# The low parts of the attention weights: an accumulating DMA in place of a GpSimd subtraction

## The chip, the cores and the metric

The kernel runs on one core of one Trainium2 chip. The metric is the device time of one execution in microseconds (us), as the median of several runs. Five engines are spoken of: TensorE (PE in the profile, with PEld for its loading of weights), VectorE (DVE), ScalarE (ACT), GpSimd (POOL) and SyncE (SP), which issues DMA transfers. Each engine works through its own list of instructions in order.

## The reference

The program is a first transformer block (sparse attention beside a gated linear recurrence, then a feed-forward network) followed by two layers of a second block (feed-forward, four mixers, feed-forward), on 512 tokens of width 1024 in float32. What matters for this change is that it is a long sequence of products of the tokens with weights that are each used once, and that between some of them stand attention stages:

```
h = _rmsnorm(x, norm1_g)
proj = h @ w_in
...                                  # queries, keys, values, gates, recurrence
attn = _nsa(q, k_cmp, v_cmp, k_slc, kv[:, :, 3], k_win, kv[:, :, 5], nsa_g)
merged = merge_g[:, :, 0] * (attn @ w_o_attn) + merge_g[:, :, 1] * (lru @ w_o_lru)
x = x + merged @ w_out
...
for l in range(DEPTH_2):
    x = x + 0.5 * swiglu(rms_norm(x, ffn1_norm[l]), ffn1_w_gate[l], ffn1_w_up[l], ffn1_w_down[l])
    h = rms_norm(x, mix_norm[l])
    pa, pb, pc, pd = jnp.split(h @ w_in[l], IN_SPLITS, axis=-1)
    ...                              # four mixers: ya, yb, yc, yd
    x = x + jnp.concatenate([ya, yb, yc, yd], axis=-1) @ w_out[l]
    x = x + 0.5 * swiglu(rms_norm(x, ffn2_norm[l]), ffn2_w_gate[l], ffn2_w_up[l], ffn2_w_down[l])
    x = rms_norm(x, final_norm[l])
```

## The kernel before

Float32 products are made of three products in the type float32r, which TensorE takes at its full rate: a number is split into a high part `hi` (the number rounded to float32r) and a low part `lo` (the number less `hi`), and the product is x_hi·w_hi + x_lo·w_hi + x_hi·w_lo. These are the three matmuls on lines 150 to 152 (`feat`, weights as the stationary or loaded operand) and on lines 180 to 182 (`tok_`, tokens as the rows of the result).

Weights come through `stream` (line 116). A DMA on SP's queue (line 126) loads four slices of 128x256, 512 KB, into a tile `raw`, of which there are two in turn. For each half of it, ScalarE writes `hi` (line 133) and another engine writes `lo` as `raw` less `hi` (line 135). There are four `hi` and four `lo` tiles in turn, so that one call of `stream` with eight slices fills the whole ring; the next call's first tile has to wait until TensorE has read the tile four places before it. A `raw` tile is free for the next load when both of its halves have been split.

Which engine writes `lo` hangs on `self.attends`. It is false in the feed-forward networks, the merge and the output projection, where VectorE does it. It is true in the three attention stages, where POOL does it: the loop over 32 units of head and branch in `nsa` (from line 1644), and the loop over 16 heads in `mix` (from line 563 to 1292), which runs once in each of the two layers. In these stages projections, gates and output projections for what comes next are put between the steps of the heads: `Fill.pump` issues them one slice at a time, at lower priority. A head's step is: scores on TensorE, minimum or maximum on VectorE, exponential on ScalarE, reciprocal on VectorE, scaling on POOL (lines 782, 958, 1106, 1585), transposes on TensorE, a split by ScalarE and VectorE (lines 219, 220), and the product with the values on TensorE.

The order of the instructions on each engine is set by a scheduler when the program is built. It goes by priorities (`tc.high_priority`: a weight load is moved up by 6000, its split by 3000, fills are moved back by 300) and by a timeline that it models. A changed instruction can therefore change the order of others.

Of the kernel before, what the change touches and what calls it, by code (L numbers as in the profile page):

```python
# [8 lines left out]
FT = mybir.dt.float32  # L9
FR = mybir.dt.float32r  # L10
I32 = mybir.dt.int32
AF = mybir.ActivationFunctionType
OP = mybir.AluOpType
# [79 lines left out]
class Kern:  # L93
# [22 lines left out]
    def stream(self, src, K, C):  # L116

        nc, tc = self.nc, self.tc
        parts = []
        st = max(1, min(4, 1024 // C))  # L120
        sp = max(1, st // 2)
        for h in range(0, K, st):
            n = min(st, K - h)
            raw = self.wp.tile([128, 1024], FT, tag="raw", name="raw", bufs=2)
            with tc.high_priority(offset=6000):
                nc.sync.dma_start(raw[:, :n * C], src[:, h * C:(h + n) * C])
            for i in range(0, n, sp):
                c = min(sp, n - i) * C
                hi = self.wp.tile([128, 512], FR, tag="hi", name="hi", bufs=self.wb)
                lo = self.wp.tile([128, 512], FR, tag="lo", name="lo", bufs=self.wb)  # L130
                x = raw[:, i * C:i * C + c]
                with tc.high_priority(offset=3000):
                    nc.scalar.activation(hi[:, :c], x, AF.Copy)  # L133
                    eng = nc.gpsimd if self.attends else nc.vector
                    eng.tensor_tensor(lo[:, :c], x, hi[:, :c].bitcast(FT), op=OP.subtract)  # L135
                for j in range(min(sp, n - i)):
                    parts.append((hi, lo, j * C))

        def get(k, a=0, b=C):
            hi, lo, o = parts[k]  # L140
            return hi[:, o + a:o + b], lo[:, o + a:o + b]
        return get
# [1690 lines left out]
```

## Time and profile before

| what | us |
|---|---|
| median of 3 runs (lowest, highest) | 3132.08 (3131.34, 3133.15) |
| the profiled execution, own time | 3132.92 |
| its span | 3131.1 |
| PE busy in the span | 3030.5 |
| VectorE, ScalarE, POOL busy in the span | 1721.3, 1389.4, 736.7 |

The 1.8 us between the profiled execution's time and its span lie outside the recorded program. The busy shares are means over the whole span: 97% for PE, 55% for VectorE, 44% for ScalarE and 24% for POOL. POOL's work is nearly all in the three attention stages, so its share has to be read stage by stage. The stretches used here for the stages are 100 to 500 us (first block), 1390 to 1760 us and 2400 to 2760 us (the mixers of the two layers). Granted clock is the share of full speed that TensorE was given.

### The profile page before, as it was taken

The page shows a single profiled execution, that of the slowest core. Times are in us where ns is not written, and L with a number is a line of the kernel's source. Part 1 is how long each engine was busy: PE and PEld are TensorE (multiplying, and loading weights), DVE is VectorE, ACT ScalarE, POOL GpSimd, SP SyncE. Part 2 cuts the span into 40 slices and gives each one's busy share as a digit, 9 for nine tenths or more (in the row PEclk, how much of TensorE's full clock was granted, in tenths as well). Part 3 has the DMA queues.
Part 4 walks back from the last instruction along what each step waited for, and adds up shares of the span by engine and source line. Part 5 has one row for each costly group of instructions (what it writes and reads, how often), then busy time and mean ns, then how long its engine had stood idle before and what let it go on. Part 6 is the DMA issues. An engine that isn't in the chain of part 4 may idle for free.

```text
span 3131.1 us, 41177 instructions
## 1 busy us (share of the span) xinstructions
PE 3030.5 (97%) x15289; PEld 2549.3 (81%) x15289; DVE 1721.3 (55%) x3167; ACT 1389.4 (44%) x2707; POOL 736.7 (24%) x699
## 2 busy tenths in 40 slices
PE   7999999999999999999888999999999998999998
PEld 6888877888888888889877888888888987778886
DVE  7576785454444454337786554355443488665433
ACT  4577774343333333236765333333332577543322
POOL 0466650010000000028853000010000877210000
PEclk9999999999999999999989999999999998999999
DMA  4311112342333323333211323323233321122232
GB/s 135 105 60 58 48 41 76 100 143 95 100 98 91 101 95 95 101 112 100 79 32 41 101 95 98 99 89 99 97 96 97 111 90 47 41 88 94 95 101 81
DMA packets 105265, 275.81 MB, mean 88 GB/s; under 512 B 27172, under 2 KB 36900, under 8 KB 104904
## 3 DMA queue, kind: packets, MB, share of 16 engines
q1 hardware_dynamic: 105064, 273.18, 28.1%
q8 instruction: 120, 1.97, 0.3%
q14 instruction: 81, 0.66, 0.1%
HBM read 268.93 MB, written 6.80 MB: 88 GB/s over the span
## 4 chain that ended last, share of the span: by engine, by line
PE 73%; issue 13%; DVE 7%; ACT 3%; POOL 3%; DMA 1%; SPq 0%; DVEq 0%; POOLq 0%; ACTq 0%
PE ps_mm L150 7%; PE ps_mm L152 7%; PE ps_mm L151 7%; PE ps_s L151 6%; PE ps_s L150 6%; PE ps_s L152 6%; PE ps_t L152 6%; PE ps_t L150 6%; PE ps_t L151 6%; PE ps_mm L180 2%; PE ps_mm L181 2%; PE ps_mm L182 2%; DVE PTl L220 1%; PE ps_t L792 1%; POOL lo L135 1%
## 5 line engine op out<-in xcount | busy, mean ns | idle before, releaser
L133 ACT ACTIVATE hi<-raw 128x512 fp32r<-128x512 f32 (+4 forms) x952 | 594.5, 627 | 1362.0 <-PE ps_mm L151 410.5
L135 DVE TENSOR_TENSOR lo<-raw,hi 128x512 fp32r<-128x512 f32 (+1 forms) x782 | 547.0, 701 | 934.1 <-ACT hi L133 925.5
L150 PE MATMUL ps_mm<-xh,hi 128*128 128x512 f32 x784 | 309.8, 395 | 1.4 <-ACT hi L133 1.2
L152 PE MATMUL ps_mm<-xh,lo 128*128 128x512 f32 x784 | 307.0, 394 | 3.1 <-POOL lo L135 3.1
L151 PE MATMUL ps_mm<-xl,hi 128*128 128x512 f32 x784 | 307.7, 392 | 0.0
L233 POOL TENSOR_TENSOR acc<-acc,sq 128x512 f32<-128x512 f32 x42 | 62.5, 1488 | 1037.8 <-issue 525.7
L152 PE MATMUL ps_s<-xh,lo 128*128 128x512 f32 (+1 forms) x664 | 259.7, 392 | 6.3 <-DVE lo L135 6.3
L150 PE MATMUL ps_s<-xh,hi 128*128 128x512 f32 (+1 forms) x664 | 256.9, 392 | 7.4 <-ACT hi L133 7.4
L151 PE MATMUL ps_s<-xl,hi 128*128 128x512 f32 (+1 forms) x664 | 260.6, 392 | 3.0 <-DVE xl L238 2.9
L181 PE MATMUL ps_mm<-lo,xh 128*128 128x256 f32 (+1 forms) x896 | 255.9, 288 | 2.0 <-DVE lo L135 2.0
L180 PE MATMUL ps_mm<-hi,xh 128*128 128x256 f32 (+1 forms) x896 | 255.4, 289 | 1.3 <-ACT tk L661 1.0
L182 PE MATMUL ps_mm<-hi,xl 128*128 128x256 f32 (+1 forms) x896 | 253.7, 286 | 0.1
L135 POOL TENSOR_TENSOR lo<-raw,hi 128x512 fp32r<-128x512 f32 (+2 forms) x170 | 225.5, 1334 | 114.6 <-ACT hi L133 107.9
L150 PE MATMUL ps_t<-xh,hi 128*128 128x512 f32 x608 | 236.9, 390 | 0.0
L151 PE MATMUL ps_t<-xl,hi 128*128 128x512 f32 x608 | 236.7, 389 | 0.0
L152 PE MATMUL ps_t<-xh,lo 128*128 128x512 f32 x608 | 235.9, 390 | 0.3 <-DVE lo L135 0.3
L152 PEld LDWEIGHTS ps_mm<-xh,lo 128*128 128x128 f32 x784 | 148.2, 189 | 35.1 <-POOL lo L135 4.1
L180 PEld LDWEIGHTS ps_mm<-hi,xh 128*128 128x128 f32 x896 | 171.9, 193 | 5.0 <-issue 1.7
L181 PEld LDWEIGHTS ps_mm<-lo,xh 128*128 128x128 f32 x896 | 172.5, 193 | 4.0 <-DVE lo L135 2.5
L150 PEld LDWEIGHTS ps_mm<-xh,hi 128*128 128x128 f32 x784 | 148.6, 190 | 32.9 <-ACT hi L133 1.9
L182 PEld LDWEIGHTS ps_mm<-hi,xl 128*128 128x128 f32 x896 | 171.9, 193 | 1.7 <-DVE xl L238 0.5
L151 PEld LDWEIGHTS ps_mm<-xl,hi 128*128 128x128 f32 x784 | 148.7, 190 | 30.1
(526 smaller groups left out, 6646.7 us busy)
## 6 DMA issues: line engine op xcount, KB each, us to landing
raw<-in_w_g SPq DMA_DIRECT2D x110, 512.0 KB
raw<-in_w_u SPq DMA_DIRECT2D x110, 512.0 KB
raw<-in_w_d SPq DMA_DIRECT2D x108, 512.0 KB
raw<-in_w_o SPq DMA_DIRECT2D x24, 512.0 KB
raw<-in_w_c SPq DMA_DIRECT2D x16, 512.0 KB
raw<-in_w_m SPq DMA_DIRECT2D x16, 512.0 KB
raw<-in_w_a SPq DMA_DIRECT2D x12, 512.0 KB
raw<-in_w_d SPq DMA_DIRECT2D x20, 256.0 KB
```

What stands on the lines that cost most here:

```text
L133: nc.scalar.activation(hi[:, :c], x, AF.Copy)
L135: eng.tensor_tensor(lo[:, :c], x, hi[:, :c].bitcast(FT), op=OP.subtract)
L150: mm(ps, wh, mh(km), start=s, stop=False)
L151: mm(ps, wh, ml(km), start=False, stop=False)
L152: mm(ps, wl, mh(km), start=False, stop=e)
L180: mm(out[tb], h, wh, start=k == 0 and tb % 2 == 0, stop=False)
L181: mm(out[tb], h, wl, start=False, stop=False)
L182: mm(out[tb], o, wh, start=False, stop=k == K - 1 and tb % 2 == 1)
L220: self.nc.vector.tensor_sub(lo, src, hi.bitcast(FT))
L233: (eng or nc.gpsimd).tensor_tensor(acc, acc, sq, op=OP.add)
L792: PE.transpose(ps[:, qb * 128:qb * 128 + 128], P[qb][:, kb * 128:kb * 128 + 128], ident)
```

## The change

Where `self.attends` is true, POOL's subtraction is taken out. ScalarE writes a second time from `raw`, with the scale -1.0, into `lo`, which then holds the negated high part. A DMA issued on POOL's queue then adds `raw` to `lo` in place (`accum_op=OP.add`). In the other stages nothing is changed in the source.

```diff
--- before.py
+++ after.py
@@ -131,8 +131,11 @@
                 x = raw[:, i * C:i * C + c]
                 with tc.high_priority(offset=3000):
                     nc.scalar.activation(hi[:, :c], x, AF.Copy)
-                    eng = nc.gpsimd if self.attends else nc.vector
-                    eng.tensor_tensor(lo[:, :c], x, hi[:, :c].bitcast(FT), op=OP.subtract)
+                    if self.attends:
+                        nc.scalar.activation(lo[:, :c], x, AF.Copy, scale=-1.0)
+                        nc.gpsimd.dma_start(lo[:, :c], x, accum_op=OP.add)
+                    else:
+                        nc.vector.tensor_sub(lo[:, :c], x, hi[:, :c].bitcast(FT))
                 for j in range(min(sp, n - i)):
                     parts.append((hi, lo, j * C))
```

The lines below 134 move down by up to three; the added DMA is line 136. The places below are in the first block's attention, where the projection of the recurrence for the next head group is filled in. In these rows `hi`, `lo` and `raw` are the weights' tiles, and the numbers count the program's tiles, so that the same tile has another number in the two programs: `hi_3386`, `hi_3390`, `hi_3396`, `hi_3400` before are `hi_3414`, `hi_3419`, `hi_3426`, `hi_3431` now; the low part's number is one higher.

ScalarE's list before at this refill of the ring (P: exponentials of the softmax, PTh: high parts of the transposed probabilities):

```order
L133 ACTIVATE hi_3386<-raw_3384 128x512
L133 ACTIVATE hi_3390<-raw_3384 128x512
L219 ACTIVATE PTh_2737<-ps_t_2734 128x256
L219 ACTIVATE PTh_2765<-ps_t_2763 128x128
L219 ACTIVATE bdh_3643<-bdr_3641 128x512
L1583 ACTIVATE P2_3025,st4_2960<-P2_3025,st4_2960 128x384
L133 ACTIVATE hi_3396<-raw_3394 128x512
L133 ACTIVATE hi_3400<-raw_3394 128x512
```

ScalarE's list now at the same place:

```order
L133 ACTIVATE hi_3414<-raw_3412 128x512
L1586 ACTIVATE P0_2988,st4_2984<-P0_2988,st4_2984 128x128
L135 ACTIVATE lo_3415<-raw_3412 128x512
L222 ACTIVATE PTh_2757<-ps_t_2754 128x256
L133 ACTIVATE hi_3419<-raw_3412 128x512
L135 ACTIVATE lo_3420<-raw_3412 128x512
L133 ACTIVATE hi_3426<-raw_3424 128x512
L135 ACTIVATE lo_3427<-raw_3424 128x512
L222 ACTIVATE bdh_3675<-bdr_3673 128x512
L1586 ACTIVATE P2_3049,st4_2984<-P2_3049,st4_2984 128x384
L222 ACTIVATE PTh_2785<-ps_t_2783 128x128
```

Three writes of a low part stand among the writes of the high parts, each in front of softmax work that was next in the list before.

TensorE's list before, from the first use of the ring's first tile to the first use of the second tile's low part:

```order
L150 MATMUL ps_mm_3405<-xh_96,hi_3386 128x512
L151 MATMUL ps_mm_3405<-xl_97,hi_3386 128x512
L152 MATMUL ps_mm_3405<-xh_96,lo_3387 128x512
L150 MATMUL ps_mm_3405<-xh_96,hi_3386 128x512
L151 MATMUL ps_mm_3405<-xl_97,hi_3386 128x512
L152 MATMUL ps_mm_3405<-xh_96,lo_3387 128x512
L150 MATMUL ps_mm_3405<-xh_96,hi_3390 128x512
L151 MATMUL ps_mm_3405<-xl_97,hi_3390 128x512
L152 MATMUL ps_mm_3405<-xh_96,lo_3391 128x512
```

TensorE's list now, from inside the first tile's use to the first use of the second tile's low part:

```order
L155 MATMUL ps_mm_3437<-xh_96,lo_3415 128x512
L153 MATMUL ps_mm_3437<-xh_96,hi_3419 128x512
L154 MATMUL ps_mm_3437<-xl_97,hi_3419 128x512
L153 MATMUL ps_mm_3438<-xh_96,hi_3414 128x512
L154 MATMUL ps_mm_3438<-xl_97,hi_3414 128x512
L155 MATMUL ps_mm_3438<-xh_96,lo_3415 128x512
L153 MATMUL ps_mm_3438<-xh_96,hi_3414 128x512
L154 MATMUL ps_mm_3438<-xl_97,hi_3414 128x512
L155 MATMUL ps_mm_3438<-xh_96,lo_3415 128x512
L153 MATMUL ps_mm_3438<-xh_96,hi_3419 128x512
L154 MATMUL ps_mm_3438<-xl_97,hi_3419 128x512
L155 MATMUL ps_mm_3437<-xh_96,lo_3420 128x512
```

The matmuls of both result banks on the first tile are now done before the second tile's low part is read: from the first use of the first tile's high part to the first use of the second low part it was 8 matmuls and is 16.

## Rows read from the trace of the kernel before

**Rows 1.** page, costliest groups; columns: busy us, mean ns, idle before and its releasers
```profile
L133 ACT ACTIVATE hi<-raw 128x512 fp32r<-128x512 f32 (+4 forms) x952 | 594.5, 627 | 1362.0 <-PE ps_mm L151 410.5
...
L135 POOL TENSOR_TENSOR lo<-raw,hi 128x512 fp32r<-128x512 f32 (+2 forms) x170 | 225.5, 1334 | 114.6 <-ACT hi L133 107.9
```

**Rows 2.** windows, attention; columns: stretch, length, PE, PEld, DVE, ACT, POOL, clock, DMA share, GB/s
```profile
100.00:500.00 400.00, 382.22 (x2240) 322.41 (x2239) 285.20 (x766) 282.71 (x661) 223.50 (x231) 0.98 0.18 57
1390.00:1760.00 370.00, 343.05 (x2147) 300.61 (x2146) 259.13 (x506) 227.06 (x481) 217.12 (x204) 0.96 0.24 71
2400.00:2760.00 360.00, 338.69 (x2113) 297.13 (x2112) 244.93 (x480) 218.98 (x469) 217.76 (x206) 0.96 0.24 72
```

**Rows 3.** what PE waited for, 100:500: us in total, times, longest
```profile
PE ps_mm L152 <- POOL lo L135: 3.1, 3, 1.2
...
PE ps_s L1384 <- ACT hi L133: 1.5, 1, 1.5
...
PE ps_mm L150 <- ACT hi L133: 1.0, 1, 1.0
```

**Rows 4.** what PE waited for, 1390:1760
```profile
PE ps_mm L1146 <- DVE kvl L1149: 2.9, 1, 2.9
PE ps_s L1027 <- ACT P L780: 1.9, 3, 1.4
...
PE ps_mm L150 <- ACT yhl L1236: 1.5, 1, 1.5
```

**Rows 5.** chain of waits, 1550:1570: start us, us, what
```profile
1555.42 1.41 POOL lo L135
...
1557.20 4.75 DMA raw<-in_w_o
1561.97 0.63 ACT hi L133
```

**Rows 6.** chain of waits over the whole span, two of its DMA transfers
```profile
1.18 3.06 DMA xk<-in_xT
...
2568.78 1.75 DMA E<-rpd
```

**Rows 7.** timeline of POOL, two writes of a low part: start us, us
```profile
271.88 1.73 POOL L135 TENSOR_TENSOR lo<-raw,hi 128x512 fp32r<-128x512 f32 x1
...
1563.74 1.28 POOL L135 TENSOR_TENSOR lo<-raw,hi 128x512 fp32r<-128x512 f32 x1
```

**Rows 8.** timeline of PE, the first use of those two low parts
```profile
273.66 0.50 PE L152 MATMUL ps_mm<-xh,lo 128*128 128x512 f32 x1 [1.17 <-POOL lo L135]
...
1609.47 0.63 PE L152 MATMUL ps_mm<-yhl,lo 128*128 128x512 f32 x2
```

**Rows 9.** SP's load instructions on line 126: ns min/median/max, first and last start
```profile
L126 SPq DMA_DIRECT2D raw<-in_w_d x128: 327/328/333, 895.1 to 3095.0; - x128
```

**Rows 10.** what the load queue waited for, whole span
```profile
SPq L126 <- POOL lo L135: 582.5, 75, 31.6
```

**Rows 11.** windows inside the two mixers, columns as in rows 2
```profile
1540.00:1580.00 40.00, 33.92 (x232) 30.73 (x230) 28.87 (x71) 28.72 (x71) 33.70 (x41) 0.91 0.28 76
1580.00:1620.00 40.00, 34.22 (x162) 26.46 (x160) 35.00 (x66) 26.64 (x59) 29.05 (x25) 0.87 0.07 19
2560.00:2600.00 40.00, 37.13 (x274) 35.67 (x274) 24.12 (x63) 23.20 (x55) 37.52 (x43) 0.87 0.28 78
2600.00:2640.00 40.00, 34.60 (x195) 29.10 (x194) 35.01 (x79) 32.38 (x77) 32.31 (x37) 0.87 0.20 57
```

**Rows 12.** groups on VectorE, 1390:1760: busy us, mean ns, idle before
```profile
L135 DVE TENSOR_TENSOR lo<-raw,hi 128x512 fp32r<-128x512 f32 x24 | 19.7, 825 | 15.4 <-ACT hi L133 13.1 <-PE ps_t L152 2.2
```

**Rows 13.** groups on VectorE, 500:900
```profile
L135 DVE TENSOR_TENSOR lo<-raw,hi 128x512 fp32r<-128x512 f32 x147 | 104.1, 708 | 172.0 <-ACT hi L133 170.9
```

## The prediction

> **What bounds the kernel now.** I read the busy times by stretch first, then what TensorE waits for in the stretches the change touches, then the chain of waits, then single instructions.
>
> By stretch, TensorE is busy in 382.22 of 400 us, 343.05 of 370 and 338.69 of 360 [rows 2]. So the kernel is bound by TensorE even in its attention stages, and those hold 17.8 + 27.0 + 21.3 = 66 us of TensorE idle time, plus what a granted clock of 0.98, 0.96 and 0.96 costs. Everything the change can gain lies in that; what it can lose has no such limit. POOL is busy in 223.5, 217.1 and 217.8 us of these stretches, ScalarE in 282.7, 227.1 and 219.0 [rows 2]: POOL is not the fullest engine over a stage, ScalarE is ahead of it in all three. In short places it is otherwise: inside the mixers POOL is busy in 33.70, 37.52 and 32.31 us of 40, and there TensorE is idle for 6.1, 2.9 and 5.4 us and its clock falls to 0.91 and 0.87 [rows 11].
>
> TensorE's waits on the instruction that goes are small: 3.1 us, three times, in the first block [rows 3]; none of the mixer's listed waits names it [rows 4]. But it also stands in longer chains. Just after a POOL subtraction of 1.41 us that starts at 1555.42 us, a load of a `raw` tile starts; it takes 4.75 us, a ScalarE write stands waiting for it with the latent's split queued behind it [rows 5], and TensorE waits 2.9 us for that split [rows 4].
>
> **The change part by part.** The 170 subtractions on POOL go: 1.334 us each, 225.5 us in all [rows 1]. In their place come 170 writes on ScalarE, 170 DMA issues on POOL's queue, and the transfers.
>
> *ScalarE.* 170 x 0.627 us, the mean of the like write of `hi` [rows 1], is 107 us more; as nearly all of it falls in the three stretches, ScalarE goes from 729 to about 836 of 1130 us [rows 2]. It is in order: behind each added write wait exponentials and splits of the softmax, as in the changed list, and for those wait VectorE and TensorE. TensorE's listed waits on ScalarE are 1.5 + 1.0 us [rows 3] and 1.9 + 1.5 us [rows 4], 5.9 us in all. ScalarE's free time falls from 401 to 294 us; were waits to grow as free time shrinks (x1.36), that is +2 us. I take 2; the ends are 0, if the scheduler finds room, and 12, twice the waits listed.
>
> *The latency of the low part.* Before: POOL's 1.33 us. Now: an issue on POOL's queue and a transfer. The trace has neither, so both are bounded. For the issue, a load's instruction on SP takes 0.33 us [rows 9], the replaced POOL instruction 1.33; I take the middle, 0.83. For the transfer, 24 KB took 1.75 us, a tile of the same 256 KB 3.06 us [rows 6], and 512 KB 4.75 us [rows 5]; the accumulation also reads the target, so the last is a bound for its bytes. I take 3.06, the nearest. The low part is then later by D = 0.83 + 3.06 - 1.33 = 2.56 us, with ends 0.33 + 1.75 - 1.33 = 0.75 and 1.33 + 4.75 - 1.33 = 4.75. The Trainium skill (DMA: Bandwidth & Descriptors, Anatomy of one DMA) fits a POOL-queue DMA as 2.0 us plus bytes over 436 GB/s, which is 2.6 us here, less than the row's 3.06; by it D would be 2.1 and the next term 10 us instead of 14. No row here shows a POOL-queue DMA.
>
> What does a later low part cost? I paired 169 low parts with the first matmul that reads them. The gap from the one's end to the other's start runs from nothing (271.88 + 1.73 = 273.61, read at 273.66, with TensorE waiting) to 44.45 us (1563.74 + 1.28 = 1565.02, read at 1609.47) [rows 7, 8]. Of the 169, 11 are under 1 us, 26 under 2, 38 under 3, 52 under 4; half are under 6.7. Most of the delay is thus hidden by the ring of four tiles. The shortfalls do not simply add: a stall also puts off the refills after it, while tiles already in flight gain by it. So I walked the pairs in order: a read is put off by the larger of the delay so far and (the delay at the read four tiles before, plus D less the gap, where that is positive). The walk gives 5 us at D = 1, 15 at 2, 21 at 2.5 and 42 at 4.
>
> The scheduler gives part of it back. In the place shown, the second tile's low part is read 16 matmuls after the first tile's first use instead of 8. TensorE makes 6500 matmuls in these 1130 us [rows 2], 0.174 us each; with each gap changed by the matmuls that the new order puts more or fewer between a tile's last read and its successor's first, the walk gives 3 us at D = 1, 9 at 2, 14 at 2.5, 19 at 3 and 47 at 5. I take 14; the ends of D give 2 and 43.
>
> *The load queue.* It waited for POOL's subtraction 75 times, 582.5 us [rows 10], so each load starts as soon as a `raw` tile is split, and will start D later. The load runs ahead of the split, under the same four tiles, and hides there; where it does not, as at 1557 us, the 2.9 us wait becomes up to 5.5. I count this inside the 14.
>
> *POOL.* Its 225.5 us of subtractions become 170 x 0.83 = 141 us of issues, 84 us less; the ends are 56 (170 x 0.33) and 227. The scaling of the softmax behind them comes sooner. That is worth something only where POOL is full and TensorE starves: the four windows of rows 11 hold 6.1 + 5.8 + 2.9 + 5.4 = 20 us of idle TensorE. As the issues free little over a third of the subtractions' time and ScalarE takes on more in the same windows, I take a quarter, 5 us; the ends are 0 and 20. A waiting DMA holds POOL's queue as the subtraction did (107.9 us behind ScalarE [rows 1]): no change.
>
> **The sum** against the profiled execution: 3132.92 + 14 + 2 - 5 = 3144 us. The median of the runs is 0.84 us under that execution, so the forecast is 3143 us. About 0.2%, 6 us, is what a measurement tells from no change; this lies beyond it.
>
> **The rivals.**
>
> *POOL was the brake in the mixers (faster).* Place: the full stretches of rows 11. Price: if the relief brings back half of their 20 us of idle time and half of what the low clock costs there (40 us x (0.09 + 0.13 + 0.13 + 0.13) = 19 us), that is -20; with late refills of 3 us the time is 3115. It decides if the issue costs POOL well under 0.8 us and D is about 1. For it: POOL is at 84% to 94% in two windows, and VectorE's subtraction of the same shape takes 0.825 us in the mixer [rows 12] against 0.708 us where POOL is nearly idle [rows 13]. Against it: TensorE is also idle for 5.8 us of 40 where POOL has 11 us free (1580 to 1620) [rows 11]. The Trainium skill (SBUF — State Buffer, Who interferes with whom) says that a VectorE instruction with two inputs in SBUF contends with a POOL instruction that reads SBUF; rows 12 and 13 agree, and by it VectorE gains too, off the bound.
>
> *The ring hides it (same).* If D is near 1, the stalls are 3 us, with 2 for ScalarE and 5 from POOL: 3132. For it: half of the gaps exceed 6.7 us, and the order was laid anew around the transfer. Against it: 26 gaps under 2 us.
>
> *The accumulating transfer is dear (much slower).* It reads two streams; at D = 4.75 the walk gives 43 us, POOL gains nothing, ScalarE takes 2: 3177. Idle TensorE goes with a lower clock in this trace (0.87 in three of rows 11), so it may be more. Against it: the DMA engines are only 18% to 24% busy in these stretches [rows 2].
>
> **How the numbers follow.** The forecast has 0.35 (its own range 3136 to 3155), the dear transfer 0.17, no change 0.22, POOL as the brake 0.26. Slower by over 0.2% is 0.35 + 0.17 = 0.52; same 0.22; faster 0.26. For 8 times in 10 the range runs from the faster rival, 3115, to a little past the dear one, 3182: each side leaves out about a tenth.
>
> **What will show it.** On POOL, 170 issues in place of subtractions, and their time: 0.83 us each, or near one end. For D: waits of TensorE on these DMAs on lines 155 and 184, some 14 us or more with what follows from them, where 3 stood. On ScalarE, 170 writes of 0.63 us. In the windows of the mixers: whether POOL's share falls below 80%, and whether TensorE's idle time and clock there go with it. I am wrong if TensorE hardly waits for the DMA (then D or the order was misjudged), or if its idle time shrinks at POOL's full stretches (then the brake was POOL).

## The result and the profile after

The changed kernel takes 3177.12 us (median of 4 runs, 3175.14 to 3179.68), the kernel before 3132.61 us beside it: a ratio of 1.0143, 95% interval 1.0127 to 1.0159. It is slower by 44.5 us. The forecast was 3143 us; the time lies inside the range and on the forecast's side, but four times as far from the time before as the likeliest case had it.

The page of the kernel after: busy times, one DMA queue, and the groups that answer to [rows 1] (columns as there).

```profile
PE 3043.1 (96%) x15289; PEld 2554.5 (80%) x15289; DVE 1715.3 (54%) x3167; ACT 1471.1 (46%) x2877; POOL 657.4 (21%) x699
...
q0 software_dynamic: 24480, 43.53, 8.1%
...
L184 PE MATMUL ps_mm<-lo,xh 128*128 128x256 f32 (+1 forms) x896 | 258.0, 290 | 14.5 <-DMA lo<-raw 12.5
...
L136 POOL DMA_DIRECT2D lo<-raw x170 | 155.6, 952 | 177.3 <-ACT lo L135 170.3
```

The first thing to see is what did not get shorter: POOL's 225.5 us of subtractions are now 155.6 us of issues, so POOL is 70 us freer, and the kernel is slower all the same. TensorE now waits 12.5 us on the new transfers on one line; the forecast had some 14 us of such waits. The loss is 44.5 us, so most of it is not in these waits themselves. Between the two profiled executions (spans of 3131.1 and 3173.4 us) TensorE is idle for 29.7 us more, and busy for 12.6 us more (3043.1 against 3030.5) with the same 15289 matmuls.

The same three stretches as [rows 2], in the kernel after:

```profile
100.00:500.00 400.00, 378.71 (x2205) 318.30 (x2203) 272.39 (x743) 302.11 (x699) 189.04 (x231) 0.97 0.42 96
1390.00:1760.00 370.00, 334.83 (x2073) 292.56 (x2072) 239.96 (x482) 242.58 (x521) 196.31 (x207) 0.94 0.46 106
2400.00:2760.00 360.00, 330.74 (x2089) 290.89 (x2088) 225.50 (x454) 234.76 (x508) 190.28 (x202) 0.97 0.48 113
```

POOL falls by 34, 21 and 27 us, and TensorE's idle time rises from 66 to 86 us. The DMA engines' share about doubles, from 0.18 and 0.24 to 0.42, 0.46 and 0.48.

What TensorE waited for in 1390:1760, two lines (the same view as [rows 4]; us in total, times, longest):

```profile
PE ps_mm L184 <- DMA lo<-raw: 6.6, 8, 1.4
PE ps_mm L1149 <- ACT tq L664: 4.2, 1, 4.2
```

The chain of waits at the start of the first mixer, of the kernel after (start us, us, what):

```profile
1403.79 0.62 ACT lo L135
...
1404.70 8.57 DMA lo<-raw
...
1415.29 0.49 ACT hi L133
1415.78 5.16 DMA raw<-in_w_c
...
1422.48 0.58 POOL lo L136
1423.06 6.67 DMA lo<-raw
1429.85 3.64 DMA raw<-in_w_c
...
1434.52 0.85 POOL lo L136
...
1435.56 7.90 DMA lo<-raw
```

Here 31.9 of 40 us are transfers, one behind the other. The first accumulation releases TensorE, whose reading lets ScalarE write the next `hi`, and then a load starts. From 1423 us on the transfers follow each other directly: the accumulation ends, its `raw` tile comes free, the next load starts, and its tile is accumulated in turn. The accumulations take 6.7 to 8.6 us here.

### The profile page after: what moved, and what is told of

It reads as the page before. It is cut to its first block, busy times and chain, and to the rows that moved or that the text cites. A ratio compares the mean times of both kernels' runs of the same rounds, so it can differ in the third digit from the quotient of the medians.

```text
span 3173.4 us, 41606 instructions
## 1 busy us (share of the span) xinstructions
PE 3043.1 (96%) x15289; PEld 2554.5 (80%) x15289; DVE 1715.3 (54%) x3167; ACT 1471.1 (46%) x2877; POOL 657.4 (21%) x699
## 3 DMA queue, kind: packets, MB, share of 16 engines
q0 software_dynamic: 24480, 43.53, 8.1%
## 4 chain that ended last, share of the span: by engine, by line
PE 80%; DVE 6%; ACT 5%; DMA 4%; issue 2%; POOL 2%; SPq 1%; DVEq 0%; POOLq 0%; ACTq 0%
PE ps_mm L153 8%; PE ps_mm L154 8%; PE ps_mm L155 8%; PE ps_t L155 7%; PE ps_s L154 7%; PE ps_s L155 7%; PE ps_s L153 7%; PE ps_t L154 7%; PE ps_t L153 7%; DMA lo<-raw 2%; PE ps_mm L184 2%; PE ps_mm L183 2%; PE ps_mm L185 2%; DMA raw<-in_w_c 1%; PE ps_t L1601 1%
## 5 line engine op out<-in xcount | busy, mean ns | idle before, releaser
L236 POOL TENSOR_TENSOR acc<-acc,sq 128x512 f32<-128x512 f32 x42 | 65.5, 1560 | 1036.2 <-issue 525.7
L184 PE MATMUL ps_mm<-lo,xh 128*128 128x256 f32 (+1 forms) x896 | 258.0, 290 | 14.5 <-DMA lo<-raw 12.5
L136 POOL DMA_DIRECT2D lo<-raw x170 | 155.6, 952 | 177.3 <-ACT lo L135 170.3
```

What stands on the lines that cost most here:

```text
L136: nc.gpsimd.dma_start(lo[:, :c], x, accum_op=OP.add)
L184: mm(out[tb], h, wl, start=False, stop=False)
L236: (eng or nc.gpsimd).tensor_tensor(acc, acc, sq, op=OP.add)
```

## The experiments

Every ratio is to the kernel before, run beside it on the same chip. In the rows marked "own" the scheduler laid the order of all engines anew; in the last four it was held, as told there.

| kernel | order | us | change | 95% interval of the ratio |
|---|---|---|---|---|
| after | own | 3177.1 | +44.5 | 1.0127 to 1.0159 |
| act_only | own | 3171.3 | +39.2 | 1.0108 to 1.0136 |
| lat | own | 3151.0 | +18.9 | 1.0048 to 1.0073 |
| hold | own | 3155.0 | +22.9 | 1.0059 to 1.0084 |
| plain | own | 3158.6 | +26.5 | 1.0066 to 1.0094 |
| act_dummy | own | 3186.4 | +55.7 | 1.0159 to 1.0188 |
| alt | own | 3156.9 | +26.1 | 1.0064 to 1.0094 |
| ob_aft | of before | 3195.9 | +65.6 | 1.0197 to 1.0225 |
| oa_bef | of after | 3144.5 | +14.2 | 1.0033 to 1.0058 |
| ob_dum | of before | 3143.1 | +12.9 | 1.0027 to 1.0052 |
| ob_act | of before | 3145.1 | +14.9 | 1.0030 to 1.0058 |

(nosim_b and nosim_a, 3309.6 and 3312.4 us, have a base of their own.) No kernel tried beats the one before.

**act_only**: the second ScalarE write stays, POOL adds, nothing is transferred.

```diff
-                        nc.gpsimd.dma_start(lo[:, :c], x, accum_op=OP.add)
+                        nc.gpsimd.tensor_tensor(lo[:, :c], x, lo[:, :c].bitcast(FT), op=OP.add)
```

> The changed kernel with the accumulating DMA taken back: ScalarE still writes the negated high part a second time, and POOL adds the raw tile to it. It keeps the 170 writes on ScalarE and leaves the transfers out. Theory 1 (the low part and the raw tile come free later by the transfer): 3130 to 3140 us, near the kernel before. Theory 2 (ScalarE's 107 us more hold up the softmax): 3150 us or more, most of the 44 us. Theory 3 (the transfers crowd the loads on the DMA engines): as theory 1.

Measured: 3171.3 us. Nearly the whole loss, without any transfer. Taken by itself this would have made ScalarE's write the cause. It is the reading that the held orders below overturned.

**lat**: the kernel before, with a plain transfer of `lo` onto itself behind POOL's subtraction, on SP's queue, so that the low part alone is to be late.

```diff
                     eng.tensor_tensor(lo[:, :c], x, hi[:, :c].bitcast(FT), op=OP.subtract)
+                    if self.attends:
+                        nc.sync.dma_start(lo[:, :c].bitcast(FT), lo[:, :c].bitcast(FT))
```

> The kernel before with one DMA more for each of the 170 low parts in the attention stages: after POOL's subtraction the low part is copied onto itself by a plain DMA on SP's queue, so that its readers wait for a transfer of 256 KB; the raw tile is free as before, and ScalarE writes nothing more. Theory 1: the low part late by about 3 to 4 us costs 10 to 25 us (3143 to 3157). If only the raw tile's late release counts: within 6 us of the kernel before. Theory 2: no change.

Measured: 3151.0 us; TensorE waits 15.4 us for these transfers:

```profile
PE ps_mm L154 <- DMA lo<-lo: 8.2, 3, 4.6
...
PE ps_mm L183 <- DMA lo<-lo: 7.2, 6, 2.1
```

A later low part is paid for by TensorE's own waits; the size is mixed with a new order. It is mixed with the queue too: the added transfers stand on SP's queue between the loads, and there they wait 309.5 us in all for POOL's subtractions (404.5 us in `hold`), so that what stands behind them on this queue is held as well. In part this replaces the loads' own waits for POOL, 582.5 us before [rows 10] and 243.8 in `lat`.

**hold**: the kernel before, with a plain transfer of the raw half onto itself behind the subtraction, so that the `raw` tile alone is to come free late.

```diff
+                    if self.attends:
+                        nc.sync.dma_start(x, x)
```

> The kernel before with one DMA more for each split of a raw tile in the attention stages: after the subtraction the half of the raw tile is copied onto itself by a plain DMA on SP's queue, so that the tile comes free for the next load only when that has landed; the low part is ready as before. My prediction held that the ring hides this: within 6 us of 3132. If the two raw tiles are the ring that runs dry in the bursts (the chain of the changed kernel goes from the low part's transfer to the next load and back): 10 to 25 us slower.

Measured: 3155.0 us. No low part is later in the code, and it costs as much as `lat`. That speaks against my part on the load queue, which had a `raw` tile's later release hidden. The order is again a new one, and the copies hold SP's queue as in `lat`, so it is a hint and not a price.

**plain**: the changed kernel with a copy in place of the accumulation. The low part is then the whole weight, so the output differs from the reference.

```diff
-                        nc.gpsimd.dma_start(lo[:, :c], x, accum_op=OP.add)
+                        nc.gpsimd.dma_start(lo[:, :c], x)
```

> The changed kernel with a plain copy in place of the accumulation on POOL's queue (the low part is then the whole weight, so the sum is not the reference's); the second ScalarE write and everything else stay. Theory 3 (the accumulation itself is dear, 6 to 9 us to landing in the bursts because it reads two streams): 15 to 30 us faster than the changed kernel, 3147 to 3162, with a median to landing of about 3 us in place of 4.1. If any transfer of this size on this queue costs the same: 3170 to 3180.

Measured: 3158.6 us, a loss of 26.5 us instead of 44.5: 18 us less than with the accumulation. The queue's line and the transfers, of `plain`:

```profile
q0 software_dynamic: 24480, 43.53, 4.6%
```

```profile
L136 POOL DMA_DIRECT2D lo<-raw x170: 530/578/771, 119.9 to 2739.7; - x170
...
DMA to landing us min/median/max: 2.1/2.6/7.5
```

and of the kernel after:

```profile
L136 POOL DMA_DIRECT2D lo<-raw x170: 850/878/2577, 120.0 to 2753.0; - x170
...
DMA to landing us min/median/max: 2.8/4.1/9.2
```

The bytes are the same 43.53 MB. Added up instead of copied they take 8.1% of 16 engines instead of 4.6%, or 0.081 x 3173.4 / 170 = 1.51 us of all engines for each transfer instead of 0.046 x 3159.6 / 170 = 0.85; the median from issue to landing is 4.1 us instead of 2.6, the issue on POOL 0.88 us instead of 0.58. The Trainium skill (DMA: Bandwidth & Descriptors, Anatomy of one DMA) fits a POOL-queue DMA as 2.0 us plus bytes over 436 GB/s, by estimate 2.6 us for 256 KB. The copy's median of 2.6 us agrees, the accumulation's 4.1 us does not, and the measurement decides.

**act_dummy**: the kernel before, with a second ScalarE write that nothing reads.

```diff
                     nc.scalar.activation(hi[:, :c], x, AF.Copy)
+                    if self.attends:
+                        du = self.wp.tile([128, 512], mybir.dt.bfloat16, tag="du", name="du", bufs=1)
+                        nc.scalar.activation(du[:, :c], x, AF.Copy, scale=-1.0)
```

> The kernel before, with a second ScalarE write per tile in the attention stages (the raw half times -1, into a scratch tile that nothing reads); POOL subtracts as before. It puts the 107 us on ScalarE and leaves the way to the low part as it was. Theory load (ScalarE's queue is what the change overfills): nearly the whole loss of the kernel with the second write alone, 3160 to 3172 us. Theory serial (the loss there came from the low part standing behind two ScalarE writes in a row): 3132 to 3142 us, as my forecast's +2 for ScalarE had it. In between: both count.

Measured: 3186.4 us, more than the whole change. By the expectation this would confirm that ScalarE is overfilled. But this kernel does less than the changed one and is slower; that raised the question whether the order had done it.

**nosim_b, nosim_a**: both kernels, the scheduler without its simulated timeline.

```diff
-    with tile.TileContext(nc, schedule_with_timeline_sim=True) as tc:
+    with tile.TileContext(nc, schedule_with_timeline_sim=False) as tc:
```

> The kernel before with the order laid by the scheduler without its simulated timeline. By itself it says nothing of the change; it is the base for the next one. I expect it slower than before, 3140 to 3250 us.

> The changed kernel with the same setting as the base just before it, where the change moves fewer rows of the order (on TensorE about half as many). Theory order (the loss comes from how the timeline scheduler laid the work anew): the difference to that base is small, under 15 us. Theories load and serial: the difference is again 35 to 55 us.

Measured: 3309.6 us (3303.2 to 3313.1) and 3312.4 us (3310.4 to 3321.4). In this looser order the change costs 3 us, less than the runs spread. That speaks for theory order as it was written, but the base holds so much waiting that a late low part may hide in it. Inconclusive.

**alt**: every second tile as in the changed kernel, the others as before.

```diff
+                    if self.attends and i:
+                        nc.scalar.activation(lo[:, :c], x, AF.Copy, scale=-1.0)
+                        nc.gpsimd.dma_start(lo[:, :c], x, accum_op=OP.add)
+                    else:
+                        eng = nc.gpsimd if self.attends else nc.vector
+                        eng.tensor_tensor(lo[:, :c], x, hi[:, :c].bitcast(FT), op=OP.subtract)
```

> Half of the change: in the attention stages every second tile (the second half of each raw tile) has its low part by ScalarE and the accumulating transfer, the other by POOL as before. If the cost is by piece (ScalarE's writes, transfers' engine time): half the loss, 3150 to 3158 us. If what decides is the one late low part per raw tile (the raw tile comes free with the last of its halves): nearly the whole loss, 3165 to 3177. If the loss comes only once ScalarE or the transfers pass some fullness: 3130 to 3142, and this could be a version that beats both.

Measured: 3156.9 us, a little over half the loss, again in an order of its own. Half of the change is not free, and this is no better version.

**The held orders.** The next four kernels end in a table: for each engine the order in which it is to issue its instructions, taken from another kernel, and drawn as one edge from each instruction to the next on its engine. Nothing else differs: in the traces each engine's instructions stand in the order that was taken, apart from the added writes. `ob_aft`, `ob_dum` and `ob_act` have the order of the kernel before, with an added ScalarE write just behind its tile's first write and the transfer (or POOL's add) where POOL's subtraction stood. `oa_bef` has the order of the changed kernel, without the added writes.

```diff
     with tile.TileContext(nc, schedule_with_timeline_sim=True) as tc:
         Kern(tc, I, out).run()
+        impose(tc, nc)
...
+        q = [by[e][k + v] for k, v in enumerate(d)]
+        for a, b in zip(q, q[1:]):
+            tc.add_manual_dep(b, a.name, dep, reason="order")
```

**ob_aft** (the changed kernel's operations in the order of before):

> The changed kernel, its instructions held on every engine in the order of the kernel before; the added ScalarE write stands just behind its tile's first write, the transfer where POOL's subtraction stood. Theory load and latency (the added work and the later low part cost the time, wherever they stand): 3165 to 3190 us, as in the changed kernel or a little more. Theory order (the loss comes from how the scheduler laid the other work anew): 3125 to 3145 us.

**oa_bef** (the operations of before in the changed kernel's order):

> The kernel before, its instructions held on every engine in the order of the changed kernel, without the added writes. Theory order: most of the loss stays though nothing was added, 3160 to 3180 us. Theory load and latency: 3128 to 3145 us. If both are wrong in part, the two runs share the loss, and their sum over the time before is near 45 us.

**ob_dum** (`act_dummy` in the order of before):

> The kernel before in its own order, with the second ScalarE write into a scratch tile that nothing reads, just behind the first. With the order laid anew this cost 55 us. Theory load: again 40 to 60 us, 3172 to 3190. Theory order: 3132 to 3145, near the +2 us that the forecast had for ScalarE.

**ob_act** (`act_only` in the order of before):

> In the order of the kernel before: ScalarE writes the negated half into the low part just behind the high part, and POOL adds the raw half to it, with no transfer. The low part is one ScalarE write later than in the kernel before, about 0.6 us. Theory transfer (in the held order the 53 us beyond ScalarE's load come from the transfer's length): 3140 to 3152 us, the dummy's +13 with 2 or 3 us for a low part that is 0.6 us later. Theory ScalarE in the way (the low part's write stands in ScalarE's queue and holds what is behind it, or comes late itself): 3165 to 3190 us.

Measured: +65.6, +14.2, +12.9 and +14.9 us. With the order held, the effects come apart:

- ScalarE's 170 writes: 12.9 us (`ob_dum`; 8.5 to 16.3 by the interval), not the 55.7 of `act_dummy`. The kernel before, held in its own order by such edges, was not run; after the first block `ob_dum` is only 0.3 us late, so the edges by themselves cost next to nothing there.
- the low part standing behind that write, 0.6 us later: 2 us more (`ob_act`), within what the runs spread.
- the transfer in place of POOL's add: 65.6 - 14.9 = 50.7 us (an estimate from the two intervals: some 6 us either way), with whatever POOL's freer time gives back already in it.
- the scheduler's laying the order anew: 44.5 - 65.6 = -21 us. The new order suits the transfers; for the old operations it is 14.2 us worse (`oa_bef`). So in the changed kernel's own order all the new operations together cost 44.5 - 14.2 = 30.3 us; how these divide between the writes and the transfer was not run, and the 50.7 us hold for the order of before.

The sum is 12.9 + 2.0 + 50.7 - 21.1 = 44.5; it comes out by construction, as the last term is what is left. So theory load falls as the main cause, and theory order in its strong form too (the old order made the change worse, not free); theory transfer stands.

Where the 50.7 us go (47.5 between the two profiled executions) can be read exactly, since `before`, `ob_act` and `ob_aft` issue the same instructions on VectorE in the same order. I paired VectorE's instructions of the three timelines (some 2850 rows each) and took how much later each one starts than before:

| before, at us | 120 | 200 | 340 | 460 | 1380 | 1440 | 1560 | 1760 | 2440 | 2560 | 2760 |
|---|---|---|---|---|---|---|---|---|---|---|---|
| ob_act later by | 1.4 | 1.0 | 1.9 | 3.3 | 2.0 | 3.5 | 7.0 | 7.4 | 6.6 | 12.1 | 14.3 |
| ob_aft later by | 0.7 | 9.4 | 9.9 | 16.4 | 15.0 | 28.2 | 33.4 | 35.3 | 36.7 | 57.2 | 61.4 |
| difference | -0.7 | 8.4 | 8.0 | 13.1 | 13.0 | 24.7 | 26.4 | 27.9 | 30.1 | 45.1 | 47.1 |

Of 47 us, 9.1 + 5.1 + 11.7 + 15.0 = 41 arise in four places, 120 to 200, 340 to 460, 1380 to 1440 and 2440 to 2560; the rest of the kernel cost 6. One of them, the first 50 us of the first mixer, columns as in [rows 2] (the stretch starts later where the kernel got there later); first before:

```profile
1390.00:1440.00 50.00, 49.79 (x410) 48.91 (x409) 19.98 (x35) 27.37 (x51) 42.84 (x32) 1.00 0.38 113
```

then `ob_act`:

```profile
1392.00:1442.00 50.00, 49.31 (x404) 48.33 (x403) 18.96 (x33) 33.01 (x63) 41.94 (x32) 1.00 0.40 115
```

then `ob_aft`:

```profile
1405.00:1455.00 50.00, 42.21 (x308) 40.90 (x307) 11.24 (x22) 24.66 (x47) 28.11 (x23) 0.90 0.71 159
```

TensorE, full before, gets through 308 matmuls instead of 410: it is idle for 7.8 us, and its granted clock is 0.90, which over 50 us is worth another 5. In this stretch of `ob_aft` it waits three times for an accumulation (us in total, times, longest):

```profile
PE ps_mm L184 <- DMA lo<-raw: 7.6, 3, 4.8
```

The longest is the first, as its chain shows; the matmul at 1415.42 is the one that reads the new low part:

```profile
1405.15 0.70 DVE xT L552
...
1406.14 0.63 ACT lo L135
...
1407.05 8.32 DMA lo<-raw
1415.42 0.58 PE ps_mm L184
```

What follows the wait is dear too. The matmul at 1415.42 in the timeline, with its wait before it:

```profile
1415.42 0.58 PE L184 MATMUL ps_mm<-lo,xh 128*128 128x256 f32 x1 [4.76 <-DMA lo<-raw]
```

and the 9 us from there on, in which the clock is at the lower of its two levels, 1.2 of 2.4 GHz (0.50):

```profile
1415.00:1424.00 9.00, 8.58 (x40) 8.59 (x41) 0.16 (x1) 1.51 (x4) 2.38 (x3) 0.50 0.56 138
```

Before the wait of 4.76 us such matmuls start 0.12 us apart, after it 0.21. The same over the whole kernel, the busy times on the page of `ob_act` (span 3145.5 us):

```profile
PE 3038.1 (97%) x15289; PEld 2554.3 (81%) x15289; DVE 1723.2 (55%) x3167; ACT 1470.3 (47%) x2877; POOL 735.8 (23%) x699
```

and of `ob_aft` (span 3193.0 us):

```profile
PE 3052.7 (96%) x15289; PEld 2564.4 (80%) x15289; DVE 1712.5 (54%) x3167; ACT 1471.3 (46%) x2877; POOL 651.4 (20%) x699
```

Of the 47.5 us, 32.9 are more idle time of TensorE and 14.6 are longer busy time for the same matmuls; the mean granted clock falls from 0.981 to 0.976.

How long a transfer takes depends on what else the DMA engines carry. In `ob_aft` in 1405:1455, with the DMA share of 0.71:

```profile
DMA to landing us min/median/max: 3.3/3.8/8.3
```

and in 1580:1760, where the share is 0.27:

```profile
DMA to landing us min/median/max: 3.1/3.4/6.1
```

The shortest is the same 3.1 to 3.3 us in both; the long ones come where loads run beside, which is where TensorE needs the tile at once. The packets in the traces bear this out. In the kernel after, 57 of the 170 accumulations had no packet of SP's queue beside them; their median is 3.3 us, whether or not an earlier accumulation was still in flight. Where SP's packets filled over 40% of the engines' time beside them (18), it is 5.6 us, and the longest is 9.2. In `ob_aft` it is 3.3 us (66) against 5.9 (16). The loads lengthen as well: the `raw` loads that ScalarE waited for in the attention stages took 3.9 us at the median in `ob_act` (9 of them) and 4.7 in `ob_aft` (16).

## Why the forecast was right in sign and wrong in size

*ScalarE, +2 us.* The busy time was right, 170 x 0.612 = 104 us more against 107, as the added write's group in the kernel after shows:

```profile
L135 ACT ACTIVATE lo<-raw 128x512 fp32r<-128x512 f32 (+2 forms) x170 | 103.8, 612 | 33.2 <-DMA raw<-in_w_o 7.5 <-PE ps_mm L184 7.5 <-DMA raw<-in_w_c 7.5
```

The price was not: 12.9 us with the order held, just over the upper end of 12. The step that failed is "were waits to grow as free time shrinks (x1.36)": in the first mixer of `ob_dum` (1390:1760) TensorE's largest wait on ScalarE nearly doubled, from the 1.9 us of [rows 4]. Over the whole kernel TensorE's idle time grew by 5.6 us and its busy time for the same matmuls by 4.6, which the forecast had at nothing. By VectorE's starts `ob_dum` is 0.3 us late after the first block, 3.2 after the first mixer and 9.3 after the second: nearly all of the price is in the mixers.

```profile
PE ps_s L1030 <- ACT P L783: 3.5, 4, 2.2
```

*The low part's latency, D = 2.56 us and +14.* The issue, 0.88 us at the median, was near my 0.83. The transfer was not my 3.06 behind the issue; landing came 4.1 us after the issue's start, which holds the issue. What I left out is ScalarE's own write, for which the transfer waits: 0.61 us. So D = 0.61 + 4.1 - 1.33 = 3.4 us at the median, and 0.61 + 3.5 - 1.33 = 2.8 in `ob_aft`. By my walk, in the held order, 2.8 us (between 21 us at 2.5 and 42 at 4) would be some 25 us; measured were 2 + 50.7. The size of D thus explains less than half of this cost. Two things that the walk leaves out are on record. It gave every tile one D, but the transfers run from 2.8 to 9.2 us, and the long ones sit at the projections, where the gaps are short. And it put the clock that falls after a wait at nothing (only the rival of the dear transfer names it, without a price): TensorE's idle time grew by 32.9 us, and the longer busy time added 14.6. In the changed kernel's own order the walk does better: at 3.4 us it gives some 25 us (between 19 at 3 and 47 at 5), where all the new operations cost 30.3.

*The load queue, "hides there".* This step failed: the chain from 1423 to 1443 above goes from an accumulation through the load that it held back to the next accumulation, for which TensorE waits. The queue's waiting, [rows 10], in the kernel after:

```profile
SPq L126 <- DMA lo<-raw: 674.6, 84, 29.9
```

A `raw` tile now comes free only when its accumulation has landed. There are two of them, so at the start of a projection the loads and the accumulations form one loop, and both run longer there than alone, as shown above. I had seen such a chain of one load [rows 5], and counted it as one wait of 2.9 us that could become 5.5. How much of the 50.7 us is the late low part and how much the late `raw` tile, no run separates: both end with the same transfer. `hold` hints only that the latter is not free.

*The scheduler gives part back.* Right, and more than I had: the walk gave 21 - 14 = 7 us, the runs 21. I did not count that the new order has a price of its own, 14.2 us for the old operations; the 21 are net of it. In the forecast's sum this is a term that was left out, as large as the one for the late low part.

*POOL, -5 us.* Its issues were forecast at 141 us and took 155.6. No gain is to be seen: in the stretches above POOL is freer, and TensorE waits more. The relief was not run alone, so a small gain inside the 50.7 us stays possible. With it falls the rival "POOL was the brake", which needed TensorE's idle time to shrink with POOL's.

*The rival "the accumulating transfer is dear"* had 3177 us, and that is the time measured. Its mechanism was the right one in the main: a longer transfer, and more waiting than the chance of 0.17 granted it. That two streams make it longer fits the 1.51 us of the engines against 0.85, but is not shown by it. Its sum agrees partly by accident: it put D at 4.75 where 3.4 was measured, ScalarE at 2 and the order's own price at nothing. My argument against it, that the DMA engines are only 18% to 24% busy, was a stage's mean; in 1390:1440 the share before was already 0.38, and in the kernel after, in the same 50 us of the mixer, it is 0.80:

```profile
1403.00:1453.00 50.00, 45.17 (x353) 43.61 (x353) 15.58 (x27) 28.98 (x55) 32.34 (x28) 0.97 0.80 175
```

*Left open.* Why `act_only` and `act_dummy` lose 24 and 43 us more in the order that the scheduler laid for them than in the held one: their orders were not run with the old operations. And how much of the transfer's price is the accumulation: 18 us between `after` and `plain`, but in two different orders.

## What to carry to other kernels

When a scheduler lays the order anew for every edit, two variants differ by their order too; here that moved the time by between -21 and +43 us, and it made a write that costs 13 us in a held order look like the whole cause. Hold the order and change the operations, then hold the operations and change the order. And price an added transfer in the stretch where its tile is needed at once, with the DMA share of that stretch and with the buffer that it keeps from being loaded, not with a stage's mean; and look at the granted clock after each wait, not at the wait alone.

## What the runs showed of the hardware

- An accumulating DMA of 256 KB within SBUF took 4.1 us from issue to landing at the median (3.5 in `ob_aft`), a copy of the same bytes on the same queue 2.6; the accumulation took 1.51 us of all 16 DMA engines, the copy 0.85, and its issue held POOL for 0.88 us against 0.58.
- Beside loads, at a DMA share of 0.71 (`ob_aft`) and 0.80 (after), single accumulations took 8.3 to 8.6 us; the shortest anywhere was 2.8, the longest 9.2. With no packet of SP's queue beside it the accumulation's median was 3.3 us in both orders, with SP's packets in over 40% of the engines' time 5.6 and 5.9.
- After a wait of 4.76 us (`ob_aft`, 1410 to 1415) TensorE's granted clock stood at 0.50 for some 10 us, and matmuls of 256 columns started 0.21 us apart instead of 0.12.
